# First loads in half pieces, sums of the opening moved from TensorE to VectorE, and a new order of the set-up block in a causal convolution

## Chip, cores, metric

One core of a Trainium2 chip. The metric is the device time of one launch in microseconds (us). A kernel was run 3 to 9 times beside runs of the kernel before on the same chip. The groups of experiments below ran on different chips, so each is compared with its own runs of the kernel before. Medians are given with their range, and ratios with a 95% interval.

## The reference

A causal convolution over the sequence with 8 taps, each a full 512x512 matrix:

```python
# x: (8, 4096, 512) fp32, kernel: (8, 512, 512) fp32
out = np.zeros_like(x)
for k in range(8):
    shifted = x if k == 0 else np.concatenate(
        [np.zeros((B, k, D), dtype=np.float32), x[:, :-k, :]], axis=1)
    out += np.matmul(shifted, kernel[k])
```

## The kernel before

Sequence positions are cut into 128 runs of 256, one run per partition; eight steps of all runs make one block. Instead of 8 taps x 8 steps = 64 matrix products per block, three levels of sums and differences of rows and of weights bring it down to three "nodes" of 9 products of 128x512x512, each product 4 matmuls of 128x512, 216 ns each. From here on "a product" is one such matmul of 128x512. Each node after the first begins with a copy by ScalarE, its "opening copy", by which progress is read below. From about 100 us on a steady loop runs, one node in 7.774 us, TensorE without gaps. The change leaves that loop alone.

The first 100 us are another matter. The weights and the first blocks have to arrive, and there are no sums of weights yet. So the first node (block 0, lower half) is computed directly with 64 matmuls, while loads come in one after another through the GpSimd queue (fp32 in memory, bf16 on chip). The order of every instruction is set by hand. The parts that matter, with cuts marked:

```python
    def load(out, src):
        nc.gpsimd.dma_start(out=out, in_=src)
    ...
    load(H[1:P, 4:8], xr[0:P - 1, RUN - 4:RUN, :])   # history: last 4 rows of the run before
    load_x(0, 0)                                     # first x block, rows 0 to 3
    ident = spool.tile([P, P], bf, name="ident")
    make_identity(nc, ident)                         # GpSimd: a memset and a select
    identh = ...; identn = ...                       # GpSimd: two more helpers, 0.9 us
    ...
    for r in range(2):                               # 16 matmuls on zeros: warm the array
        for k in range(4):
            fill(pair(k))
    ...
    load_w(4)
    transpose_pe("xh", 2, H, 5, 8)
    sums_pe("d4a", 1, (-4, 0), (-3, 1))   # transposes and adds in one go: matmuls that
    ...                                   # accumulate x and history rows in PSUM
    transpose_pe("x1", 2, xin[0, 1], 0, 4)
    nc.scalar.copy(out=XT[:, 4:8], in_=bank["x1"])   # x block two, evicted by ScalarE
```

A `bank` is a buffer in PSUM, into which TensorE writes here; to evict it is to copy it to SBUF. "x block two" is `xin[0, 1]`, "block three" `xin[1, 0]`; the later x tiles are transposed by DMA instead of TensorE. D4, E4 and the like are names of sums of rows; "the D4 sum behind the DMA transpose" is VectorE's first add on a tile transposed by DMA. The "warming matmuls" are the 16 on zeros.

## Time and profile before

| | before |
|---|---|
| time | 783.48 us median of 3 (783.41 to 783.87) |
| span in the profile | 780.9 us |
| first product starts | 13.81 us |
| x block two's transposes start | 25.08 us |
| 120 products done, next one starts | 48.79 us |
| 160 products done (opening copy of the fifth node) | 57.7 us |
| an opening copy early in the loop | 89.4 us |

The busy shares, the stretches, the start of TensorE's timeline and two load issues are shown in the prediction.

GpSimd's timeline at the start (start us, duration us, engine, line, what). L80 is the line of every load issue: history at 1.23, x at 1.90, then work on the identity and its helpers, then the first weights at 4.04.

```profile
1.23 0.68 POOL L80 DMA_DIRECT2D D<-in_x_dram  x1 [0.80 <-POOLq L637]
1.90 0.56 POOL L80 DMA_DIRECT2D xin<-in_x_dram  x1
...
3.53 0.54 POOL L148 TENSOR_SCALAR identn<-ident 128x128 bf16<-128x128 bf16 x1
4.04 0.82 POOL L80 DMA_DIRECT2D w<-in_kernel_dram  x1
```

### The profile page before, as it was taken

What the parts mean: (1) busy time and instruction counts of PE and PEld (TensorE: products, weight loads), DVE (VectorE), ACT (ScalarE), POOL (GpSimd) and SP (SyncE); (2) the same over time, 40 slices, a digit from 0 to 9 for tenths busy, and PEclk for the clock granted to TensorE, in tenths of its full rate; (3) what the DMA queues carried; (4) which work ended last, traced back from release to release, by engine and by line L of the source; (5) the groups of instructions that cost most, each with busy time, mean ns of one, the idle gap of its engine ahead of it and who ended that gap; (6) DMA issues with size and microseconds to landing.
All of it is one profiled execution on the core that took longest, in us unless ns stands there. A gap on an engine that the chain in (4) does not pass through costs nothing.

```text
span 780.9 us, 9507 instructions
## 1 busy us (share of the span) xinstructions
PE 767.4 (98%) x3620; PEld 349.0 (45%) x3620; DVE 659.3 (84%) x764; ACT 283.2 (36%) x460; POOL 42.8 (5%) x83
## 2 busy tenths in 40 slices
PE   7899999999999999999999999999999999999997
PEld 4444444444444444444444444444444444444443
DVE  4899888888888889888898888898888898888895
ACT  2453433333333333343324343333343333343332
POOL 5000000000000000000000000000000000000000
PEclk9999999999999999999999999999999999999999
DMA  9963979778788777878777788877787877788753
GB/s 163 210 120 114 237 176 207 169 187 167 178 179 206 174 176 173 177 184 194 184 171 168 179 190 188 191 166 179 165 187 187 195 170 182 166 172 200 179 153 123
DMA packets 159229, 138.37 MB, mean 177 GB/s; under 512 B 130130, under 2 KB 134226, under 8 KB 159184
## 3 DMA queue, kind: packets, MB, share of 16 engines
q1 hardware_dynamic: 145312, 98.84, 46.3%
q0 software_dynamic: 13728, 38.66, 31.1%
q8 instruction: 28, 0.46, 0.2%
q10 hardware_dynamic: 144, 0.26, 0.1%
q14 instruction: 17, 0.14, 0.1%
HBM read 77.32 MB, written 67.11 MB: 185 GB/s over the span
## 4 chain that ended last, share of the span: by engine, by line
PE 94%; DMA 3%; DVE 1%; POOL 1%; issue 0%; ACT 0%; DVEq 0%; POOLq 0%
PE pp L215 94%; DMA xin<-in_x_dram 2%; DMA XT<-xin 1%; POOL w L80 0%; DVE D L76 0%; PE pp L192 0%; DVE pp L76 0%; ACT XT L390 0%; DVE y L76 0%; POOL D L80 0%; DVEq L648 0%; POOL xin L80 0%; POOL identn L148 0%; PE pp L186 0%; POOL ident masks.py:199 0%
## 5 line engine op out<-in xcount | busy, mean ns | idle before, releaser
L215 PE MATMUL pp<-w,D 128*128 128x512 bf16 x3280 | 715.8, 379 | 1.7 <-DMA w<-in_kernel_dram 0.9
L215 PEld LDWEIGHTS <-D 128*128 128x128 bf16 x3280 | 320.2, 98 | 390.4 <-issue 2.8
L76 DVE TENSOR_TENSOR D<-D 128x2048 bf16<-128x2048 bf16 (+2 forms) x250 | 227.2, 948 | 3.4 <-ACT D L369 3.4
L76 DVE TENSOR_TENSOR y<-pp,ms 128x1024 f32<-128x1024 f32 (+1 forms) x121 | 146.4, 1212 | 45.3 <-PE pp L215 45.3
L76 DVE TENSOR_TENSOR D<-XT 128x2048 bf16<-128x2048 bf16 (+2 forms) x153 | 142.5, 947 | 12.1 <-DMA XT<-xin 10.4
L262 ACT COPY pp<-pp 128x512 f32<-128x512 f32 x95 | 54.1, 570 | 260.6 <-PE pp L215 260.6
L274 ACT COPY pp<-pp 128x512 f32<-128x512 f32 x95 | 54.2, 570 | 167.1 <-PE pp L215 165.6
L76 DVE TENSOR_TENSOR pp<-dts,pp 128x512 f32<-128x512 f32 x95 | 65.7, 691 | 43.9 <-ACT dts L280 42.6
L317 ACT COPY ms<-pp 128x1024 f32<-128x1024 f32 x60 | 61.0, 1016 | 35.0 <-PE pp L215 33.0
L80 POOL DMA_DIRECT2D xin<-in_x_dram x64 | 34.0, 531 | 692.5 <-DMA XT<-xin 675.8
L290 DVE SCALAR_TENSOR_TENSOR pp<-pp,dts 128x512 f32<-128x512 f32 x95 | 66.0, 695 | 3.2
L280 ACT COPY dts<-pp 128x512 f32<-128x512 f32 x95 | 57.5, 606 | 0.0
L276 ACT ACTIVATE pp<-pp 128x512 f32<-128x512 f32 x95 | 56.1, 590 | 0.8 <-PE pp L215 0.8
L215 PE MATMUL pp<-w,XT 128*128 128x512 bf16 x120 | 30.8, 379 | 0.0
L76 DVE TENSOR_TENSOR w<-w,w 128x2048 bf16<-128x2048 bf16 x19 | 22.9, 1219 | 1.5 <-DMA w<-in_kernel_dram 1.3
L215 PEld LDWEIGHTS <-XT 128*128 128x128 bf16 x120 | 11.7, 98 | 14.2
L186 PE MATMUL pp<-zero,ident 128*128 128x512 bf16 x20 | 6.7, 493 | 3.1 <-POOL ident masks.py:199 3.1
L215 PE MATMUL pp<-w,F 128*128 128x512 bf16 x36 | 8.7, 379 | 0.2 <-DVE pp L76 0.2
L215 PE MATMUL pp<-w,w 128*128 128x512 bf16 x36 | 8.3, 379 | 0.0
L192 PE MATMUL pp<-ident,xin 128*128 128x128 bf16 x48 | 3.2, 219 | 3.6 <-DMA xin<-in_x_dram 1.4
L80 POOL DMA_DIRECT2D w<-in_kernel_dram x8 | 6.1, 785 | 0.5 <-DMA w<-in_kernel_dram 0.5
L358 DVE COPY D<-pp 128x1536 bf16<-128x1536 bf16 x1 | 1.0, 958 | 6.1 <-PE pp L192 6.1
(59 smaller groups left out, 78.7 us busy)
## 6 DMA issues: line engine op xcount, KB each, us to landing
out_dram<-y SPq DMA_DIRECT2D x123, 512.0 KB, 3.4
xin<-in_x_dram POOLq DMA_DIRECT2D x64, 512.0 KB, 6.0
w<-in_kernel_dram POOLq DMA_DIRECT2D x8, 512.0 KB, 15.7
out_dram<-ms SPq DMA_DIRECT2D x2, 512.0 KB, 5.4
out_dram<-f SPq DMA_DIRECT2D x2, 512.0 KB, 6.3
XT<-xin SPq DMA_TRANSPOSE x61, 6.1
D<-in_x_dram POOLq DMA_DIRECT2D x1, 508.0 KB, 5.6
D<-in_x_dram POOLq DMA_DIRECT2D x1, 381.0 KB, 9.4
```

Of the source, the lines that this page charges most:

```text
L76: nc.vector.tensor_tensor(out=o, in0=a, in1=b, op=op)
L80: nc.gpsimd.dma_start(out=out, in_=src)
L186: nc.tensor.matmul(pw[:, h], lhsT=ident, rhs=zero, start=True, stop=True)
L192: nc.tensor.transpose(o[:, t - t0, c * P:(c + 1) * P], src[:, t, c * P:(c + 1) * P], ident)
L215: nc.tensor.matmul(bank, lhsT=comp[:, c * P:(c + 1) * P], rhs=w[:, c, :], start=start and c == 0, stop=c == DC - 1, skip_group_check=True)
L262: nc.scalar.copy(out=n.q[:, 0], in_=n.q[:, 1])
L274: nc.scalar.copy(out=n.p[b_][:, 1], in_=n.q[:, 1])
L276: nc.scalar.mul(out=n.p[b_][:, 1], in_=n.q[:, 1], mul=-1.0)
L280: nc.scalar.copy(out=n.dts, in_=n.q[:, 0])
L290: nc.vector.scalar_tensor_tensor(out=p[:, 0], in0=p[:, 1], scalar=-1.0, in1=n.dts, op0=MUL, op1=SUB)
L317: nc.scalar.copy(out=ms[b_], in_=p)
L358: nc.vector.tensor_copy(out=XF[:, 0:3], in_=bank["xh"])
```

## The change

The intent: start the first products sooner, and take work off TensorE. The first history rows and the first x block are loaded in two halves each, so that their transposes can begin when half has come. TensorE only transposes; VectorE makes the sums that TensorE made by accumulating. The two helper identities are not needed any more. The rest of the set-up block (some 200 calls) is put in a new order. The core of the diff:

```diff
-    load(H[1:P, 4:8], xr[0:P - 1, RUN - 4:RUN, :])
-    load_x(0, 0)
+    load_h(-4, -2)
+    load_x(0, 0, 0, 2)
     ident = spool.tile([P, P], bf, name="ident")
     make_identity(nc, ident)
-    identh = spool.tile([P, P], bf, name="identh")
-    ... (identh, identn made on GpSimd)
 ... (cut: mid_pe, mid_act, sums_pe removed)
+    transpose_pe("h0", 0, H, 4, 6)
+    load_h(-2, 0)
+    load_x(0, 0, 2, 4)
     load_w(4)
-    transpose_pe("xh", 2, H, 5, 8)
-    sums_pe("d4a", 1, (-4, 0), (-3, 1))
+    transpose_pe("x0", 2, xin[0, 0], 0, 2)
+    nc.vector.tensor_copy(out=XF[:, 4:6], in_=bank["x0"])
+    nc.vector.tensor_copy(out=XF[:, 0:2], in_=bank["h0"])
+    first_run(XF[:, 0:2])
+    tt(D4[:, 0:2], XF[:, 0:2], XF[:, 4:6], ADD)
 ...
     transpose_pe("x1", 2, xin[0, 1], 0, 4)
-    nc.scalar.copy(out=XT[:, 4:8], in_=bank["x1"])
+    nc.vector.tensor_copy(out=XT[:, 4:8], in_=bank["x1"])
 ... (cut: the other calls of the block in a new order)
```

More of the change, by code (lines that the diff above doesn't have):

```diff
@@ L82, with load_x @@
     xin = {}
-    def load_x(i, h):
-        xin[i, h] = xpool.tile([P, 4, D], bf, name="xin")
-        load(xin[i, h], xr[:, K * i + 4 * h:K * i + 4 * h + 4, :])
+    def load_x(i, h, a=0, b=4):
+        if a == 0:
+            xin[i, h] = xpool.tile([P, 4, D], bf, name="xin")
+        t0 = K * i + 4 * h
+        load(xin[i, h][:, a:b], xr[:, t0 + a:t0 + b, :])
     def transpose_x(i, h):
@@ L138, with load_h @@
     H = D421
-    load(H[1:P, 4:8], xr[0:P - 1, RUN - 4:RUN, :])
-    load_x(0, 0)
+    def load_h(a, b):
+        load(H[1:P, 8 + a:8 + b], xr[0:P - 1, RUN + a:RUN + b, :])
+    load_h(-4, -2)
+    load_x(0, 0, 0, 2)
     ident = spool.tile([P, P], bf, name="ident")
     make_identity(nc, ident)
-    identh = spool.tile([P, P], bf, name="identh")
-    nc.gpsimd.tensor_copy(out=identh, in_=ident)
-    nc.gpsimd.memset(identh[:, 0:P:G], 0.0)
-    identn = spool.tile([P, P], bf, name="identn")
-    nc.gpsimd.tensor_scalar_mul(out=identn, in0=ident, scalar1=-1.0)
     zero = spool.tile([P, D], bf, name="zero")
@@ L170 @@
     bank = {}
-    def mid_pe(h, k, *which):
-        o, u, v = mid(*which)
-        bank[which, h] = pair(k)
-        for c in range(2):
-            pw = bank[which, h][:, c]
-            nc.tensor.matmul(pw, lhsT=ident, rhs=u[:, 2 * h + c], start=True, stop=False)
-            nc.tensor.matmul(pw, lhsT=identn, rhs=v[:, 2 * h + c], start=False, stop=True)
-    def mid_act(h, *which):
-        nc.scalar.copy(out=mid(*which)[0][:, 2 * h:2 * h + 2], in_=bank[which, h])
     def fill(pw):
@@ L194, in transpose_pe @@
         bank[name] = o[:, 0:t1 - t0]
-    def sums_pe(name, k, *sums):
-        pw = bank[name] = pair(k)
-        for h, ts_ in enumerate(sums):
-            for c in range(DC):
-                for n, t in enumerate(ts_):
-                    src, idt = (xin[0, 0][:, t], ident) if t >= 0 else (H[:, 8 + t], identh)
-                    nc.tensor.matmul(pw[:, h, c * P:(c + 1) * P], lhsT=src[:, c * P:(c + 1) * P],
-                                     rhs=idt, start=n == 0, stop=n == len(ts_) - 1,
-                                     skip_group_check=True)
     for r in range(2):
@@ L346, with first_run @@
     C0, C1 = W[MID, HI, MID], W[MID, LO, MID]
-    load_w(4)
-    transpose_pe("xh", 2, H, 5, 8)
-    sums_pe("d4a", 1, (-4, 0), (-3, 1))
-    load(H[1:P, 1:4], xr[0:P - 1, RUN - 7:RUN - 4, :])
+    def first_run(z):
+        nc.vector.memset(z[:, :, 0:D:G], 0.0)
+    transpose_pe("h0", 0, H, 4, 6)
+    load_h(-2, 0)
+    load_x(0, 0, 2, 4)
+    load_w(4)
+    transpose_pe("x0", 2, xin[0, 0], 0, 2)
+    nc.vector.tensor_copy(out=XF[:, 4:6], in_=bank["x0"])
+    nc.vector.tensor_copy(out=XF[:, 0:2], in_=bank["h0"])
@@ L356 @@
+    first_run(XF[:, 0:2])
+    tt(D4[:, 0:2], XF[:, 0:2], XF[:, 4:6], ADD)
+    transpose_pe("xb", 2, xin[0, 0], 2, 4)
+    n0.p = {0: pair(0), 1: pair(1)}
+    transpose_pe("h1", 0, H, 6, 8)
+    nc.scalar.copy(out=XF[:, 6:8], in_=bank["xb"])
+    nc.scalar.copy(out=XF[:, 2:4], in_=bank["h1"])
+    direct(0, 0)
+    load_h(-7, -4)
+    first_run(XF[:, 2:4])
     load_w(6)
-    sums_pe("d4b", 2, (-2, 2), (-1, 3))
-    nc.vector.tensor_copy(out=XF[:, 0:3], in_=bank["xh"])
-    transpose_pe("xf", 2, xin[0, 0], 0, 4)
+    transpose_pe("he", 2, H, 1, 4)
@@ L360 @@
     load_w(5)
-    nc.vector.tensor_copy(out=D4[:, 0:2], in_=bank["d4a"])
-    nc.scalar.copy(out=D4[:, 2:4], in_=bank["d4b"])
-    n0.p = {0: pair(0), 1: pair(1)}
+    tt(D4[:, 2:4], XF[:, 2:4], XF[:, 6:8], ADD)
+    direct(0, 3)
+    direct(0, 1)
+    nc.scalar.copy(out=F0, in_=XF[:, 4])
     fill(pair(3))
-    load_w(7)
-    direct(0, 2)
-    direct(0, 1)
-    direct(0, 3)
-    nc.scalar.copy(out=XF[:, 3:7], in_=bank["xf"])
-    sums_pe("e4a", 2, (-5, -1), (-6, -2))
-    nc.vector.memset(XF[:, 0:3, 0:D:G], 0.0)
@@ L372 @@
-    tt(D2, XF[:, 0:5], XF[:, 2:7], ADD)
-    direct(2, 3)
-    tt(F21, D2[:, 0:4], D2[:, 1:5], ADD)
-    mid_dve(1, LO, HI)
-    sums_pe("e4b", 2, (-7, -3))
-    direct(1, 2)
-    direct(0, 0)
-    load_x(0, 1)
-    tt(D1, XF[:, 2:4], XF[:, 3:5], ADD)
-    mid_dve(2, LO, HI)
-    nc.scalar.copy(out=E4[:, 3:1:-1], in_=bank["e4a"])
-    mid_dve(2, LO, LO)
-    load_x(1, 0)
-    load_w(0)
-    nc.vector.tensor_copy(out=E4[:, 1], in_=bank["e4b"][:, 0])
-    direct(1, 3)
-    direct(1, 1)
-    transpose_pe("x1", 2, xin[0, 1], 0, 4)
@@ L390 @@
-    nc.scalar.copy(out=XT[:, 4:8], in_=bank["x1"])
-    load_w(2)
-    mid_dve(1, LO, LO)
-    direct(1, 0)
-    transpose_pe("x2", 2, xin[1, 0], 0, 4)
-    mid_dve(2, LO, MID)
-    load_w(1)
-    tt(D4[:, 4:8], XF[:, 3:7], XT[:, 4:8], ADD)
-    direct(2, 1)
-    nc.vector.tensor_copy(out=XT[:, 2:4], in_=bank["x2"][:, 2:4])
+    direct(0, 2)
+    direct(2, 2)
+    tt(E4[:, 1:4], bank["he"], XF[:, 1:4], ADD)
+    first_run(E4[:, 1:4])
+    tt(D2, XF[:, 1:6], XF[:, 3:8], ADD)
+    load_w(7)
+    direct(1, 0)
@@ new lines @@
+    direct(1, 3)
+    load_x(0, 1)
+    tt(D1, XF[:, 3:5], XF[:, 4:6], ADD)
+    direct(1, 2)
+    mid_dve(1, LO, HI)
+    load_x(1, 0)
+    direct(1, 1)
+    mid_dve(2, LO, HI)
+    tt(F21, D2[:, 0:4], D2[:, 1:5], ADD)
+    load_w(0)
+    mid_dve(1, LO, LO)
+    mid_dve(2, LO, LO)
+    direct(2, 3)
+    mid_dve(2, LO, MID)
+    transpose_pe("x1", 2, xin[0, 1], 0, 4)
+    nc.vector.tensor_copy(out=XT[:, 4:8], in_=bank["x1"])
+    tt(D4[:, 4:8], XF[:, 4:8], XT[:, 4:8], ADD)
+    direct(2, 0)
+    nc.scalar.copy(out=C0[:, 0:2], in_=XT[:, 6:8])
@@ L400 @@
+    prep_d41(HI)
+    transpose_pe("x2", 2, xin[1, 0], 0, 4)
+    nc.scalar.copy(out=XT[:, 2:4], in_=bank["x2"][:, 2:4])
+    load_w(2)
+    direct(3, 0)
     prep_d42(HI)
     nc.scalar.copy(out=XT[:, 0:2], in_=bank["x2"][:, 0:2])
-    nc.scalar.copy(out=C0[:, 0:2], in_=XT[:, 6:8])
+    direct(3, 3)
     tt(T4, XT[:, 4:8], XT[:, 0:4], ADD)
     direct(3, 1)
-    prep_d41(HI)
-    tt(T42[:, 0:2], D4[:, 6:8], T4[:, 0:2], ADD)
-    direct(3, 0)
-    nc.scalar.copy(out=C1, in_=XT[:, 0:4])
-    direct(2, 0)
@@ L410 @@
-    nc.scalar.copy(out=F0, in_=XF[:, 3])
-    direct(3, 3)
-    fill(pair(2))
-    tt(D41[:, 1], T4[:, 0], T4[:, 1], ADD)
-    load_w(3)
+    fill(pair(2))
+    load_w(3)
+    nc.scalar.copy(out=C1, in_=XT[:, 0:4])
+    direct(3, 2)
+    tt(D41[:, 1], T4[:, 0], T4[:, 1], ADD)
+    node_a1(1)
+    tt(D41[:, 0], D4[:, 7], T4[:, 0], ADD)
+    direct(2, 1)
+    load_w(1)
+    node_a0(nodes[1])
+    tt(T42[:, 0:2], D4[:, 6:8], T4[:, 0:2], ADD)
     tt(T42[:, 2:4], T4[:, 0:2], T4[:, 2:4], ADD)
-    node_a1(1)
@@ L417 @@
-    direct(2, 2)
+    node_u(nodes[1])
+    load_x(1, 1)
+    tt(D421[:, 0], D42[:, 7], T42[:, 0], ADD)
     node_e(nodes[0], 0)
-    tt(D41[:, 0], D4[:, 7], T4[:, 0], ADD)
-    node_a0(nodes[1])
-    node_u(nodes[1])
-    direct(3, 2)
+    node_seed(nodes[1], 0)
     mid_dve(1, HI, HI)
-    node_seed(nodes[1], 0)
     prep_d27()
+    node_v(nodes[1], 0)
+    mid_dve(2, HI, LO)
+    tt(D421[:, 1:4], T42[:, 0:3], T42[:, 1:4], ADD)
+    node_seed(nodes[1], 1)
     node_dts(nodes[1])
-    node_seed(nodes[1], 1)
@@ L428 @@
     tt(D42[:, 3], D4[:, 1], D4[:, 3], ADD)
-    node_v(nodes[1], 0)
-    tt(D421[:, 0], D42[:, 7], T42[:, 0], ADD)
-    load_x(1, 1)
-    node_v(nodes[1], 1)
-    tt(D421[:, 1:4], T42[:, 0:3], T42[:, 1:4], ADD)
-    node_a1(2)
-    mid_dve(2, HI, LO)
-    transpose_x(1, 1)
-    mid_dve(1, HI, LO)
-    node_d(nodes[1], 0)
-    node_l(nodes[1], 0, LO)
-    mid_dve(2, HI, MID)
-    nc.scalar.copy(out=D4[:, 2:4], in_=T4[:, 2:4])
-    node_d(nodes[1], 1)
-    load_x(2, 1)
-    node_e(nodes[0], 1)
-    node_u(nodes[2])
@@ L446 @@
-    node_l(nodes[1], 0, HI)
-    node_e(nodes[1], 0)
-    node_a0(nodes[2])
-    node_seed(nodes[2], 0)
-    prep_d421(HI)
-    load_x(2, 0)
-    mid_dve(2, HI, HI)
-    node_l(nodes[1], 1, LO)
-    node_l(nodes[1], 1, HI)
-    nc.scalar.copy(out=U1, in_=XT[:, 0])
+    load_x(2, 0)
+    node_d(nodes[1], 0)
+    mid_dve(1, HI, LO)
+    mid_dve(2, HI, HI)
+    node_a1(2)
+    node_l(nodes[1], 0, HI)
+    node_v(nodes[1], 1)
+    load_x(2, 1)
+    node_d(nodes[1], 1)
+    mid_dve(2, HI, MID)
+    prep_d421(HI)
@@ L456 @@
+    node_l(nodes[1], 0, LO)
+    node_a0(nodes[2])
+    node_l(nodes[1], 1, HI)
+    node_e(nodes[1], 0)
+    node_e(nodes[0], 1)
+    nc.scalar.copy(out=D4[:, 2:4], in_=T4[:, 2:4])
+    node_u(nodes[2])
+    mid_dve(0, HI, HI)
+    node_seed(nodes[2], 0)
+    node_seed(nodes[2], 1)
+    node_l(nodes[1], 1, LO)
+    node_dts(nodes[2])
+    transpose_x(1, 1)
+    nc.scalar.copy(out=D42[:, 3], in_=T42[:, 3])
     node_v(nodes[2], 0)
+    node_v(nodes[2], 1)
     prep_d4(HI)
-    nc.scalar.copy(out=D42[:, 3], in_=T42[:, 3])
@@ L459 @@
-    node_seed(nodes[2], 1)
-    node_v(nodes[2], 1)
-    node_dts(nodes[2])
-    mid_dve(0, HI, HI)
-    node_e(nodes[1], 1)
     prep_d41(HI)
     node_d(nodes[2], 0)
-    node_l(nodes[2], 0, HI)
-    tt(A1[:, 0], C0[:, 1], C1[:, 0], ADD)
-    prep_d42(HI)
-    node_d(nodes[2], 1)
-    transpose_x(2, 0)
-    mid_dve(0, LO, HI)
     node_a1(3)
     node_l(nodes[2], 0, LO)
+    mid_dve(0, LO, LO)
+    mid_dve(0, HI, LO)
+    prep_d42(HI)
+    node_l(nodes[2], 0, HI)
     node_a0(nodes[3])
+    node_d(nodes[2], 1)
@@ L475 @@
+    node_u(nodes[3])
     node_e(nodes[2], 0)
-    mid_dve(0, LO, LO)
+    node_e(nodes[1], 1)
+    node_seed(nodes[3], 0)
     tt(D421[:, 0:4], D42[:, 3:7], D42[:, 4:8], ADD)
-    node_u(nodes[3])
     node_l(nodes[2], 1, HI)
     node_seed(nodes[3], 1)
-    node_seed(nodes[3], 0)
+    mid_dve(0, LO, HI)
+    tt(A1[:, 0], C0[:, 1], C1[:, 0], ADD)
     node_dts(nodes[3])
+    node_v(nodes[3], 0)
+    node_v(nodes[3], 1)
     mid_dve(1, MID, HI)
-    node_v(nodes[3], 1)
+    node_l(nodes[2], 1, LO)
@@ L485 @@
     node_d(nodes[3], 1)
-    mid_dve(0, HI, LO)
-    node_v(nodes[3], 0)
+    node_e(nodes[2], 1)
     node_d(nodes[3], 0)
-    node_l(nodes[2], 1, LO)
+    mid_dve(1, MID, LO)
     node_a1(4)
-    mid_dve(1, MID, LO)
-    tt(D21[:, 2:4], C1[:, 0:2], C1[:, 2:4], ADD)
     node_l(nodes[3], 1, HI)
     node_l(nodes[3], 0, LO)
+    nc.scalar.copy(out=U1, in_=XT[:, 0])
+    node_a0(nodes[4])
+    tt(D21[:, 2:4], C1[:, 0:2], C1[:, 2:4], ADD)
     mid_dve(2, MID, MID)
-    node_e(nodes[2], 1)
-    load_x(3, 0)
@@ L498 @@
-    node_l(nodes[3], 0, HI)
-    node_a0(nodes[4])
-    tt(D21[:, 0:2], C0[:, 0:2], C1[:, 0:2], ADD)
-    node_u(nodes[4])
-    node_e(nodes[3], 0)
-    node_l(nodes[3], 1, LO)
-    tt(A1[:, 1], C1[:, 0], C1[:, 1], ADD)
+    node_dts(nodes[4])
+    tt(D21[:, 0:2], C0[:, 0:2], C1[:, 0:2], ADD)
+    node_l(nodes[3], 0, HI)
+    node_e(nodes[3], 0)
+    node_u(nodes[4])
+    tt(A1[:, 1], C1[:, 0], C1[:, 1], ADD)
+    node_l(nodes[3], 1, LO)
+    load_x(3, 0)
+    transpose_x(2, 0)
     mid_dve(2, MID, LO)
+    node_seed(nodes[4], 0)
@@ L506 @@
+    node_seed(nodes[4], 1)
+    node_v(nodes[4], 0)
     mid_dve(2, MID, HI)
-    node_seed(nodes[4], 0)
-    node_v(nodes[4], 0)
-    node_seed(nodes[4], 1)
-    node_dts(nodes[4])
+    node_a1(5)
     node_d(nodes[4], 0)
-    node_a1(5)
     node_v(nodes[4], 1)
+    node_l(nodes[4], 0, HI)
     prep_m()
-    node_l(nodes[4], 0, HI)
     node_l(nodes[4], 0, LO)
+    node_e(nodes[3], 1)
+    node_u(nodes[5])
+    node_d(nodes[4], 1)
     node_a0(nodes[5])
-    node_e(nodes[3], 1)
-    node_d(nodes[4], 1)
@@ L520 @@
-    node_u(nodes[5])
+    node_y(nodes[4], 0, LO)
+    node_y(nodes[4], 0, HI)
+    prep_d4(LO)
+    node_l(nodes[4], 1, HI)
+    tt(F21[:, 1], D21[:, 0], D21[:, 1], ADD)
+    node_dts(nodes[5])
+    tt(F21[:, 0], D2[:, 0], D21[:, 0], ADD)
     node_seed(nodes[5], 0)
     node_l(nodes[4], 1, LO)
-    tt(F21[:, 0], D2[:, 0], D21[:, 0], ADD)
-    node_l(nodes[4], 1, HI)
-    node_y(nodes[4], 0, LO)
-    node_y(nodes[4], 0, HI)
+    node_v(nodes[5], 0)
+    node_y(nodes[4], 1, LO)
     store(0, LO, 0, first[0, LO, 0])
-    tt(F21[:, 1], D21[:, 0], D21[:, 1], ADD)
@@ L529 @@
-    node_dts(nodes[5])
-    node_v(nodes[5], 0)
+    store(0, HI, 0, first[0, HI, 0])
+    node_d(nodes[5], 0)
     prep_d27()
     node_seed(nodes[5], 1)
-    store(0, HI, 0, first[0, HI, 0])
-    load_x(3, 1)
-    node_y(nodes[4], 1, LO)
     node_v(nodes[5], 1)
-    node_d(nodes[5], 0)
+    node_a1(6)
     node_d(nodes[5], 1)
+    transpose_x(2, 1)
+    node_y(nodes[4], 1, HI)
+    store(0, HI, 1, first[0, HI, 1])
+    node_l(nodes[5], 0, HI)
+    node_l(nodes[5], 0, LO)
     tt(F21[:, 2:4], D21[:, 1:3], D21[:, 2:4], ADD)
-    node_l(nodes[5], 0, LO)
@@ L541 @@
-    node_l(nodes[5], 0, HI)
-    node_a1(6)
-    node_l(nodes[5], 1, HI)
+    node_y(nodes[5], 0, HI)
     node_u(nodes[6])
-    prep_d4(LO)
-    store(0, LO, 1, first[0, LO, 1])
-    node_y(nodes[4], 1, HI)
-    node_a0(nodes[6])
     node_y(nodes[5], 0, LO)
     prep_d41(LO)
-    transpose_x(2, 1)
+    node_l(nodes[5], 1, HI)
     node_l(nodes[5], 1, LO)
-    store(0, HI, 1, first[0, HI, 1])
+    store(0, LO, 1, first[0, LO, 1])
     node_seed(nodes[6], 0)
+    node_a0(nodes[6])
     node_v(nodes[6], 0)
-    node_y(nodes[5], 0, HI)
@@ L557 @@
     tt(D21[:, 0:2], D2[:, 0:2], D2[:, 1:3], ADD)
-    node_dts(nodes[6])
+    store(1, LO, 0, first[1, LO, 0])
     node_seed(nodes[6], 1)
     node_v(nodes[6], 1)
+    node_dts(nodes[6])
+    prep_d42(LO)
+    node_d(nodes[6], 0)
+    store(1, HI, 0, first[1, HI, 0])
+    node_y(nodes[5], 1, HI)
+    node_a1(7)
+    load_x(3, 1)
+    node_y(nodes[5], 1, LO)
+    store(1, HI, 1, first[1, HI, 1])
+    store(1, LO, 1, first[1, LO, 1])
     tt(D21[:, 2:4], D2[:, 2:4], D2[:, 3:5], ADD)
-    node_d(nodes[6], 0)
@@ L563 @@
-    prep_d42(LO)
-    node_y(nodes[5], 1, HI)
     node_d(nodes[6], 1)
-    store(1, LO, 0, first[1, LO, 0])
-    node_y(nodes[5], 1, LO)
-    store(1, HI, 0, first[1, HI, 0])
-    node_a1(7)
-    store(1, HI, 1, first[1, HI, 1])
     prep_d4(HI)
-    store(1, LO, 1, first[1, LO, 1])
     for k, (i, a) in enumerate(order):
```

## The prediction

> **What bounds the kernel now.** I read the busy shares first, then a table of stretches, then the timeline of the first 50 us with its waits, and last the landings of single loads.
>
> ```profile
> PE 767.4 (98%) x3620; PEld 349.0 (45%) x3620; DVE 659.3 (84%) x764; ACT 283.2 (36%) x460; POOL 42.8 (5%) x83
> ```
>
> TensorE looks busy 98% of 780.9 us, but the average hides two regimes. The table of stretches shows them (columns: stretch and length, busy us and count of each engine, clock, DMA share, GB/s):
>
> ```profile
> 0.00:13.80 13.80, 9.51 (x78) 5.67 (x79) 4.36 (x5) 2.52 (x3) 6.97 (x17) 1.00 0.85 147
> 13.80:36.00 22.20, 18.57 (x126) 9.67 (x125) 17.78 (x20) 9.91 (x9) 4.62 (x7) 1.00 1.20 207
> 36.00:60.00 24.00, 23.26 (x107) 10.22 (x106) 23.48 (x28) 13.52 (x21) 1.06 (x2) 1.00 0.75 135
> ...
> 120.00:200.00 80.00, 80.00 (x372) 36.22 (x371) 69.39 (x80) 27.87 (x47) 3.70 (x7) 1.00 0.82 186
> ```
>
> From 120 us on TensorE has no gap. ScalarE's copy that opens a node (36 products of 128x512, 95 such nodes plus a first one of 64 products) comes every 7.774 us there: 216 ns a product, which nothing in this change touches. The code has 3,484 products (the trace lost 12), and 3,484 x 0.216 = 752.5 us. So 780.9 - 752.5 = 28.4 us are not products: about 4.4 us after the last one (the critical chain leaves TensorE at about 776.4), about 24 us before and between the first ones. Only these 24 us can move.
>
> The timeline shows where they lie (start us, us, engine, line; L215 are products, L192 transposes; in brackets the idle time before and what ended it):
>
> ```profile
> 8.45 0.83 PE L192 MATMUL pp<-ident,D 128*128 128x128 bf16 x12
> ...
> 13.81 2.75 PE L215 MATMUL pp<-w,D 128*128 128x512 bf16 x12
> ...
> 20.07 3.61 PE L215 MATMUL pp<-w,D 128*128 128x512 bf16 x16 [0.91 <-DMA w<-in_kernel_dram]
> ...
> 25.08 1.07 PE L192 MATMUL pp<-ident,xin 128*128 128x128 bf16 x16 [1.40 <-DMA xin<-in_x_dram]
> ...
> 26.18 1.86 ACT L390 COPY XT<-pp 128x2048 bf16<-128x2048 bf16 x1 [7.68 <-PE pp L192]
> ...
> 28.10 1.05 PE L192 MATMUL pp<-ident,xin 128*128 128x128 bf16 x16 [1.09 <-ACT XT L390]
> ```
>
> ```profile
> 45.17 1.23 DVE L76 TENSOR_TENSOR D<-XT 128x2048 bf16<-128x2048 bf16 x1 [0.52 <-DMA XT<-xin]
> ```
>
> ```profile
> 48.79 12.28 PE L215 MATMUL pp<-w,D 128*128 128x512 bf16 x56 [0.74 <-DVE pp L76]
> ```
>
> The first product starts at 13.8 us. Up to 28 us TensorE waits for loads and for ScalarE's 1.86 us eviction. From 28 to about 90 us VectorE is packed (23.48 of 24 us in one stretch) and sets the pace with TensorE; at 45.17 even VectorE waits for a DMA transpose. By 48.79 us TensorE has done 120 products, worth 25.9 us: 22.9 of the 24 us are lost by then.
>
> The loads have their own clock. Issues looked at singly (KB written, us to landing):
>
> ```profile
> D<-in_x_dram POOLq DMA_DIRECT2D x1, 508.0 KB, 5.6
> ```
>
> ```profile
> w<-in_kernel_dram POOLq DMA_DIRECT2D x1, 512.0 KB, 8.5
> ```
>
> The history rows are issued at 1.23 and land at 6.8; the first x block lands at 9.4, the first weights (issued 4.04) at 12.5, the next at 16.8, then 20.1, 22.6, x block two at 25.0, three at 27.5, and so on every 2.5 us to 40.2. One load after another, at the full 205 GB/s written: a stream that the change does not shorten.
>
> **What the Trainium skill says.**
> - "TensorE: Matmul & The Clock Gate", section "Wait — 56ns, not 53.3ns?", gives 55.6 ns start to start for 128 columns and 215.7 ns for 512 on a warm array. The trace agrees: 16 transposes in 1.05 us of which the last takes 0.219 are 55 ns apart, and a product takes 216.
> - The same page, "Part 4: PE-mode transpose", says that transposes do not count as busy for the clock gate in the way matmuls do. No run here shows it yet; it carries a rival below.
> - "VectorE: DVE Perf Modes", "The perf-mode tier table": an add of two bf16 tensors in SBUF runs at 2x (1224 ns for 2048), with any PSUM operand at 1x. The trace has 1220 ns for 128x2048.
> - "Perfetto Trace Analysis", "DMA Optimizations": splitting a transfer lets work start sooner if the DMA engines are generally idle. Here they are idle only before 3 us; the share is 0.85 to 1.20 after that, so halves bring forward the first half and nothing else.
>
> **The change part by part.**
>
> (a) Removed: 56 sum matmuls (32 for D4, 24 for E4) and 28 transposes; added: 44 transposes. 84 - 44 = 40 fewer, at 0.055 each 2.2 us of TensorE, but mostly beside waits. The two helper identities on GpSimd go (0.9 us of POOL); two more load issues of 0.6 us take their place, so the first weights are issued at about 4.3 instead of 4.0 and still land at 12.5, behind the same bytes.
>
> (b) First product. The 16 warming matmuls end at 8.2 as before. The first history half (landed by about 5.6) and first x half (6.8) are there: 16 transposes to 9.5. VectorE copies two banks of 128x1024 (0.68 each) to 10.8, then adds 128x1024 (0.69) by 12.0. The second halves transpose at 10.3 to 11.4; ScalarE evicts both (1.01 each, 0.92 apart) by 12.85, and the first product's bank is the one evicted last. Weights 12.5, eviction 12.85: first product at 12.9, 0.9 us earlier.
>
> (c) To 28.6 us. After four products (13.8) the older history rows, landing at 14.25, hold TensorE 0.5 us; 12 transposes end at 15.0; sixteen products and two fills (3.9 us) end at 18.9; the next need weights that land at 20.1: 1.2 us idle. Twenty products to 24.4, idle to 25.08 for x block two, transposes to 26.15, four products. Its eviction moves from ScalarE (1.86) to VectorE (about 1.2), done at 27.5, so the third block's transposes start when it lands, 27.55, not at 28.10, and end at 28.6, not 29.15. By then 44 products are done against 36: 8 x 0.216 + 0.55 = 2.3 us ahead.
>
> (d) What survives. Now VectorE binds. It has one 1.2 us eviction more and one 0.68 copy less, and reaches the sum T4 at 30.65 (when ScalarE's last eviction lands) against 30.99, with one 0.6 us sum already behind it. TensorE spends about 1 us waiting for ScalarE's seeds of node 1, since no product stands between "u" and the first "v" any more. VectorE's D4 sum on the DMA transpose again cannot start before 45.2 (the same load at 40.2 plus 5.0). But one 1.14 us weight difference has been moved in front of that gate. So the operand for the next product is there at about 47.7 instead of 48.75, and 128 products are done at 48.9 against 50.5: 1.6 ahead. The next weight difference needed (1,MID,HI) ends at 55.4, and TensorE, there at 54.9, waits: 40 groups of four are done at 56.3 against 57.7, 1.4 ahead.
>
> (e) 57 to 97 us. The transpose of block 2 is issued later, at about 57.5, and is due by 63.4; with 5 to 6 us it just fits. The kernel before loses 0.16, 0.36 and 0.24 us there to VectorE; the new order gives VectorE's results 1 us or more of slack, so 0 to 0.5 comes back. After 97 us the loop and the tail are the same.
>
> Sum: 1.4 + about 0.1 = 1.5 us. 783.5 - 1.5 = 782.0 us.
>
> **Rivals.**
> - The gates bind harder than I think: VectorE or the 45.2 us transpose leaves nothing, and the 2.3 us of part (c) become waiting. For it: VectorE's 23.48 of 24 us. Against it: the 1.14 us moved in front of the gate. Time 783.2 to 783.6.
> - The array goes cold. From 8.2 to 12.9 us TensorE now does only transposes and waits. At half speed for some 3.4 us (the window that the page's Part 1 gives), eight products would cost 1.7 us more. Against it: 1.7 us of waits at 20.1 and 25.1 absorb most. Time 782 to 783.5.
> - A later wait appears: the block 2 transpose lands after 64 and stops VectorE, which then delays its later sums. Time 782.5 to 784.
> - The new order fits better than my walk: no seed wait, no wait at 55, and the 2.3 us stay to the end. Time 781.
>
> **Range and chances.** The first and last rivals bound the range: 780.8 to 783.5, with 782.0 as the likeliest. 2% is 15.7 us; all losses before the loop are 24 us, and the first 12.5 of them are the load of x and weights that stays, so faster by 2% is nearly impossible, and nothing in the change can add 15 us. Chances 0.01, 0.98, 0.01.
>
> **What would show it.** First product at 12.9; waits of about 1.2 us for weights at 20.1 and 0.6 for x at 25.1; third block's transposes at 27.55; VectorE's D4 sum at 45.2 behind the DMA transpose; 128 products by 49; the nodes' opening copies in the loop about 1.5 us earlier than in the trace before; a loop of 7.774 us per node. First products paced at 430 ns, as the first warming matmuls are, a VectorE gap near 63 us, or a changed loop pace would make it wrong.

## More of the kernel before

A stretch of 2 us (busy us and counts of PE, PEld, DVE, ACT, POOL, then clock, DMA share, GB/s). The last figure matters: 207 GB/s, loads at full pace.

```profile
6.00:8.00 2.00, 2.00 (x8) 0.81 (x7) 0.00 (x0) 0.00 (x0) 2.00 (x4) 1.00 1.06 207
```

The chain of waits that ends last, in order of time (start us, length us, what). Up to 25 us it is made of the issue of x block two and its way through the queue (17.42 us behind the loads ahead of it); from 29 us it is TensorE with one detour by VectorE.

```profile
7.61 17.42 DMA xin<-in_x_dram
...
25.08 1.08 PE pp L192 x16
...
29.15 4.32 PE pp L215 x20
...
33.90 13.30 PE pp L215 x60
```

## The result, and the profile after

| | before | after |
|---|---|---|
| time, median (range) | 783.65 us (783.41 to 783.91, 6 runs) | 783.74 us (782.96 to 784.59, 6 runs) |
| first product | 13.81 | 13.63 |
| first weights have landed | 12.54 | 13.40 |
| x block two's transposes | 25.08 | 26.46 |
| x block three's transposes | 28.10 | 28.92 |
| D4 sum behind the DMA transpose | 45.17 | 46.69 |
| 120 products done, next starts | 48.79 | 48.77 |
| 160 products done | 57.7 | 58.2 |
| the opening copy that was at 89.4 | 89.4 | 89.8 |

The ratio of the times is 1.0002, with 0.9989 to 1.0015 as its interval: the same, and 1.7 us above what I predicted. Ratios here and below are the mean time of one kernel's fast runs over that of the other's fast runs of the same rounds, so they are not quite the ratio of the medians quoted. The profiled run of the changed kernel was its slowest, so its span (782.7) overstates it; what is read below lies in its first 110 us.

The busy shares show the intent fulfilled and nothing gained. TensorE has 40 operations fewer: 3,580 weight loads for 3,620, as the code has it (of the matmuls, some records are missing in this trace).

```profile
PE 764.5 (98%) x3509; PEld 347.7 (44%) x3580; DVE 660.8 (84%) x768; ACT 280.7 (36%) x459; POOL 42.8 (5%) x82
```

The chain of waits of the changed kernel, in order of time, is the key view. The same load of x block two, issued at the same time (7.55 against 7.61), takes 18.86 us instead of 17.42. And where the kernel before had TensorE on the chain from 29 us on, now it is a load again until 41.5, the DMA transpose behind it, and VectorE's sum.

```profile
7.55 18.86 DMA xin<-in_x_dram
...
26.46 1.08 PE pp L180 x16
...
27.82 13.69 DMA xin<-in_x_dram
...
41.60 5.00 DMA XT<-xin
...
46.69 1.24 DVE D L76
```

Where did the stream lose its time? Among the 2 us stretches one stands out: 118 GB/s instead of 207.

```profile
6.00:8.00 2.00, 2.00 (x6) 0.76 (x5) 0.00 (x0) 0.00 (x0) 2.00 (x4) 1.00 0.81 118
```

I added up the sizes of the load queue's packets in the order in which they ended: 512 KB are in at 6.65 us (before 6.43), but 1,024 KB at 10.15 (before 8.86): of 1.29 us, 0.22 are lost in the first half megabyte and the rest in the second, which is now the second pair of halves. Their 255 packets start between 6.4 and 10.34 us, and around 6.6 us only 9 packets are in flight on the 16 DMA engines, where before it was 16. GpSimd issued these two loads at 2.99 and 3.53, right after the identity:

```profile
2.44 0.23 POOL masks.py:197 MEMSET ident<- 128x128 bf16 x1
2.75 0.29 POOL masks.py:199 TENSOR_SCALAR_AFFINE_SELECT ident<-ident 128x128 bf16<-128x128 bf16 x1
2.99 0.55 POOL L80 DMA_DIRECT2D D<-in_x_dram  x1
3.53 0.55 POOL L80 DMA_DIRECT2D xin<-in_x_dram  x1
```

The first weights come next in the queue. They are issued at 4.07, as before (4.04), and land 9.3 us later, at 13.40, where before it was 8.5 us (shown in the prediction) and 12.54:

```profile
w<-in_kernel_dram POOLq DMA_DIRECT2D x1, 512.0 KB, 9.3
```

TensorE's start shows a second thing (L192 are products now, L180 transposes). Eight products from 16.66 take 2.88 us where a warm array needs 1.9, and twelve transposes take 1.46 instead of 0.83: the array had gone cold. The table of stretches says it in one figure, the clock 0.92, which was 1.00 in this stretch before; the trace's clock record is at one half from 15.24 to 18.66 us.

```profile
13.63 1.02 PE L192 MATMUL pp<-w,D 128*128 128x512 bf16 x3 [1.42 <-ACT D L346]
15.41 1.46 PE L180 MATMUL pp<-ident,D 128*128 128x128 bf16 x12 [0.76 <-DMA D<-in_x_dram]
16.66 2.88 PE L192 MATMUL pp<-w,D 128*128 128x512 bf16 x8
```

```profile
13.80:36.00 22.20, 20.31 (x116) 10.22 (x118) 19.10 (x23) 6.07 (x7) 3.20 (x5) 0.92 1.19 207
```

At 107.83 a third thing: VectorE waited 2.14 us for a DMA transpose that took 6.8 us from issue to landing (100.94 to 107.74), and TensorE lost 1.1 us behind it, at 109.5. In the trace before the same transpose took 5.0 us. The line before, then the line after:

```profile
105.65 1.23 DVE L76 TENSOR_TENSOR D<-XT 128x2048 bf16<-128x2048 bf16 x1 [0.35 <-DMA XT<-xin]
...
107.83 1.23 DVE L76 TENSOR_TENSOR D<-XT 128x2048 bf16<-128x2048 bf16 x1 [2.14 <-DMA XT<-xin]
```

So there were three candidates for the missing 1.5 us: the loads (my theory after reading), the cold array (a rival of the prediction), and VectorE's added work (another). The experiments test them. The late transpose is a fourth; no experiment was made for it, but the traces of all of them bear on it (see the rivals below).

### The profile page after: what moved, and what is told of

Its sections match the earlier page's. It is cut to its first block, busy times and chain, and to the rows that moved or that the text cites. A ratio compares the mean times of both kernels' runs of the same rounds, so it can differ in the third digit from the quotient of the medians.

```text
span 782.7 us, 9358 instructions
## 1 busy us (share of the span) xinstructions
PE 764.5 (98%) x3509; PEld 347.7 (44%) x3580; DVE 660.8 (84%) x768; ACT 280.7 (36%) x459; POOL 42.8 (5%) x82
## 4 chain that ended last, share of the span: by engine, by line
PE 87%; DMA 7%; DVE 4%; issue 1%; POOL 1%; ACT 0%; SPq 0%; DVEq 0%; ACTq 0%; POOLq 0%
PE pp L192 87%; DMA xin<-in_x_dram 4%; DMA XT<-xin 2%; DVE D L76 1%; DVE w L76 1%; DVE y L76 1%; POOL w L80 0%; DVE pp L76 0%; DVE pp L267 0%; ACT pp L251 0%; POOL D L80 0%; POOL xin L80 0%; PE pp L180 0%; DVE A L76 0%; SPq L277 0%
## 5 line engine op out<-in xcount | busy, mean ns | idle before, releaser
L192 PE MATMUL pp<-w,D 128*128 128x512 bf16 x3214 | 714.0, 379 | 7.1 <-ACT D L346 1.4
L192 PEld LDWEIGHTS <-D 128*128 128x128 bf16 x3280 | 320.5, 98 | 393.7 <-issue 5.1
L76 DVE TENSOR_TENSOR D<-D 128x1024 bf16<-128x1024 bf16 x252 | 228.5, 946 | 0.4 <-issue 0.2
L192 PE MATMUL pp<-w,XT 128*128 128x512 bf16 x117 | 30.5, 379 | 0.2
L192 PEld LDWEIGHTS <-XT 128*128 128x128 bf16 x120 | 11.7, 98 | 14.2
L192 PE MATMUL pp<-w,w 128*128 128x512 bf16 x35 | 9.0, 379 | 0.7 <-ACT pp L251 0.7
L192 PE MATMUL pp<-w,F 128*128 128x512 bf16 x35 | 8.4, 379 | 0.0
```

The costliest lines, as they stand in the source:

```text
L76: nc.vector.tensor_tensor(out=o, in0=a, in1=b, op=op)
L192: nc.tensor.matmul(bank, lhsT=comp[:, c * P:(c + 1) * P], rhs=w[:, c, :], start=start and c == 0, stop=c == DC - 1, skip_group_check=True)
```

## The experiments

Twelve kernels ran, in three groups of four; all gave correct results. "Block two" is the start of x block two's transposes, "160" the start of the opening copy of the fifth node (160 products done), "6–8" the GB/s in that stretch, all from the one profiled run of each. The names e1 to e12 are those that the expectations use; the medians of the kernel before were 783.51, 783.33 and 783.42 us in the three groups.

| kernel | median us (range) | ratio to before, interval | 6–8 | block two | 160 |
|---|---|---|---|---|---|
| before | 783.5 | 1 | 207 | 25.08 | 57.7 |
| after | 783.74 (782.96–784.59) | 1.0002 [0.9989, 1.0015] | 118 | 26.46 | 58.2 |
| after again (e5) | 784.11 (782.86–784.62) | 1.0009 [0.9997, 1.0022] | 101 | 26.60 | 57.8 |
| after, whole loads (e1) | 782.24 (781.81–782.59) | 0.9984 [0.9972, 0.9997] | 199 | 25.81 | 57.0 |
| before, with halves (e2) | 784.44 (783.54–784.9) | 1.0012 [0.9999, 1.0025] | 160 | 26.29 | 59.2 |
| after, array kept warm (e3) | 783.47 (783.05–783.57) | 0.9999 [0.9987, 1.0012] | 108 | 26.07 | 57.8 |
| after, all halves issued first (e4) | 782.62 (781.8–783.99) | 0.9989 [0.9976, 1.0003] | 199 | 25.28 | 56.4 |
| e4 with memsets between (e9) | 783.8 (783.42–784.14) | 1.0006 [0.999, 1.0023] | 126 | 26.15 | 57.9 |
| after, identity before the loads (e6) | 782.42 (782.19–783.72) | 0.9995 [0.9982, 1.0008] | 181 | 25.48 | 56.8 |
| before, block two evicted by VectorE (e7) | 785.45 (784.48–785.69) | 1.0024 [1.001, 1.0037] | 207 | 24.91 | 60.0 |
| e4 with 8 warming matmuls (e8) | 781.92 (781.62–782.23) | 0.9984 [0.9971, 0.9996] | 184 | 25.77 | 56.9 |
| e8 again (e12) | 781.85 (781.55–783.54) | 0.9984 [0.9969, 0.9999] | 188 | 25.35 | 56.5 |
| e6 with 8 warming matmuls (e10) | 782.43 (782.18–782.69) | 0.9987 [0.9972, 1.0002] | 161 | 26.04 | 57.4 |
| e1 with 8 warming matmuls (e11) | 781.98 (781.53–783.08) | 0.9984 [0.9969, 0.9998] | 203 | 25.66 | 57.1 |

**Group one: which part costs?** First the halves alone undone, everything else as changed:

```diff
-    load_h(-4, -2)
-    load_x(0, 0, 0, 2)
+    load_h(-4, 0)
+    load_x(0, 0)
 ...
-    load_h(-2, 0)
-    load_x(0, 0, 2, 4)
```

> The changed kernel with its first history and x rows loaded whole again, all else as changed. Theory 1 (the halves made the whole load stream 1.4 us later, and that ate the gain): x block two lands near 25.1 us instead of 26.5, the first DMA transpose starts near 40.2 instead of 41.6, the D4 sum behind it near 45.2 instead of 46.7, and the time falls by 1.0 to 1.5 us to 782.2 to 782.8. Rival A (the cold TensorE array costs it): time unchanged, 783.5 to 784. Rival B (VectorE's packed order costs it, wherever the loads land): loads land earlier, but the time stays at 783.5 to 784.

The time is 782.24 us, and the stream is whole again (199 GB/s). The chain of waits now has no second load on it: after block two's transposes comes VectorE, and it stays on the chain down to the D4 sum at 45.40, with no wait for a DMA named any more. Block two itself starts at 25.81, only 0.65 us before the changed kernel's and still 0.7 behind the kernel before, so the stretch from 6 to 8 us is not the whole of its delay.

```profile
25.81 1.08 PE pp L180 x16
...
26.91 1.24 DVE XT L378
...
28.17 1.24 DVE D L76
...
45.40 1.23 DVE D L76
```

Then the opposite: the halves alone, put into the kernel before.

```diff
-    load(H[1:P, 4:8], xr[0:P - 1, RUN - 4:RUN, :])
-    load_x(0, 0)
+    load(H[1:P, 4:6], xr[0:P - 1, RUN - 4:RUN - 2, :])
+    load_x(0, 0, 0, 2)
 ... (identity, identh, identn)
+    load(H[1:P, 6:8], xr[0:P - 1, RUN - 2:RUN, :])
+    load_x(0, 0, 2, 4)
     load_w(4)
```

> The kernel before with one thing changed: its first history and x rows loaded in halves. Theory 1: x block two lands 1.2 to 1.6 us later than 25.0 and the time rises by 1.0 to 1.6 us to 784.7 to 785.3. Rivals A and B: the halves are harmless by themselves, 783.4 to 783.9.

784.44 against 783.51 for the kernel before of the same rounds: 0.9 us lost, a little less than expected and with an interval that just reaches 1; block two is 1.2 us later. Both kernels tell the same story from two sides: the halves, as they are issued here, cost about 0.9 us in the kernel before and 1.5 in the changed one (medians of different rounds), and the rest of the change gains about 1.3. Which part of that rest gains it was not separated.

Third, the array kept warm, by 14 more matmuls on zeros in the gaps where the changed kernel waits:

```diff
     tt(D4[:, 0:2], XF[:, 0:2], XF[:, 4:6], ADD)
+    for _ in range(2):
+        fill(pair(3))
     transpose_pe("xb", 2, xin[0, 0], 2, 4)
 ... (3 more before direct(0, 0), 2 more after it)
```

> The changed kernel with 14 more matmuls on zeros in TensorE's three early gaps (10.0, 12.0 and 14.3 us), so that the array stays at full speed. Rival A: the products from 13.6 to 18.7 us go at 216 ns instead of 430, and the time falls by 1 us or more, to below 782.8. Theory 1: they go at 216 ns too, but then TensorE waits about 1.5 us longer for the weights and x block two, and the time stays within 0.3 us of the changed kernel, 783.4 to 784.1.

The edit does what it should, and the time stays at 783.47. The eight products take 1.89 us and the twelve transposes 0.83, and then TensorE waits for a load, which the cold kernel did not need to:

```profile
15.45 0.83 PE L180 MATMUL pp<-ident,D 128*128 128x128 bf16 x12
16.12 1.89 PE L192 MATMUL pp<-w,D 128*128 128x512 bf16 x8
...
21.31 1.02 PE L192 MATMUL pp<-w,w 128*128 128x512 bf16 x4 [1.15 <-DMA w<-in_kernel_dram]
```

The speed won is handed back 3 us later. The cold array was real and cost nothing measurable.

Fourth, the same four half loads, but all issued before the identity is made:

```diff
     load_h(-4, -2)
     load_x(0, 0, 0, 2)
+    load_h(-2, 0)
+    load_x(0, 0, 2, 4)
     ident = spool.tile([P, P], bf, name="ident")
     make_identity(nc, ident)
```

> The changed kernel with all four half loads issued before GpSimd makes the identity, so the third and fourth issue 0.6 us earlier. In the trace half of the DMA engines are idle from 6.2 to 7.2 us. If that is because the third load was issued too late, the gap closes, x block two lands near 25.9 instead of 26.5 and the time falls by about 0.5 us; if the gap has another cause or the halves are slow by their packets alone (2 KB packets took 180 ns, half of a 4 KB packet 162 ns), it lands at 26.3 to 26.6 and the time stays at 783.5 to 784.

```profile
2.45 0.55 POOL L80 DMA_DIRECT2D D<-in_x_dram  x1
2.98 0.54 POOL L80 DMA_DIRECT2D xin<-in_x_dram  x1
3.51 0.22 POOL masks.py:197 MEMSET ident<- 128x128 bf16 x1
```

The stream is back at 199 GB/s, 1,024 KB are in at 9.03 us (8.86 with whole loads), block two starts at 25.28 and 160 products are done at 56.4, 1.8 us before the changed kernel. So it is not the size of the pieces: a half load's packets of 2 KB took 174 to 192 ns where the whole load's of 4 KB took 324 to 333. It is where they are issued. The time, 782.62, is better, but one of its runs was at 783.99 and the interval just reaches 1.

**Group two: is it the place of the identity?** First the changed kernel once more, unedited, for the noise.

> The changed kernel once more, unedited, beside the next three on one chip. Is the slow stretch of its load stream (118 GB/s from 6 to 8 us, against 199 to 207 with whole loads) there in another execution? Theory 1: yes, within 100 to 165 GB/s, x block two lands at 26 us or later, and the time is 783.4 to 784.0. Rival: it was one execution's accident; then 190 GB/s or more, and x block two near 25.3.

784.11 us; the stretch, at 101 GB/s, is as poor as the first time. This time the array was warm without help (eight products in 1.89 us), and the time was no better for it, which is a second, unplanned answer to the cold array:

```profile
16.18 1.89 PE L192 MATMUL pp<-w,D 128*128 128x512 bf16 x8
```

Second, the identity made before any load:

```diff
-    load_h(-4, -2)
-    load_x(0, 0, 0, 2)
     ident = spool.tile([P, P], bf, name="ident")
     make_identity(nc, ident)
+    load_h(-4, -2)
+    load_x(0, 0, 0, 2)
```

> The changed kernel with the identity made before any load is issued, so that all four half loads are issued in a row, about 0.8 us later than in the run that issued them first. If the slow stretch comes from GpSimd's identity work standing between the second and third issue, it is gone (190 GB/s or more in every 2 us stretch once the loads run), and x block two lands near 26.1, 0.8 later than there. If it comes from half loads being too small to keep the queue fed, it is there again and x block two lands at 26.8 or later. Time 783.2 to 784.2 either way; the trace decides, not the time.

The four half loads are issued about 0.2 us later than with the halves first (I had expected 0.8), but without a break; the stretch has 181 GB/s, block two starts at 25.48, and the time is 782.42, against 784.11 for the unedited kernel in the same rounds. Two of my figures were missed: the stretch stays under 190 GB/s, and the time is below 783.2. The spread of both is wide (783.72 the slowest here, 782.86 the fastest there), so this one pair settles it in the trace rather than in the time.

Third, one part of the change alone in the kernel before: block two's bank evicted by VectorE.

```diff
     transpose_pe("x1", 2, xin[0, 1], 0, 4)
-    nc.scalar.copy(out=XT[:, 4:8], in_=bank["x1"])
+    nc.vector.tensor_copy(out=XT[:, 4:8], in_=bank["x1"])
```

> The kernel before with one part of the change alone: x block two's bank of 128x2048 is evicted by VectorE (about 1.2 us) instead of ScalarE (1.86 us). If the gain that whole loads set free comes from this shorter path to block three's transposes, they start at 27.6 instead of 28.1 and the time falls by 0.4 to 0.6 us, to 782.9 to 783.2. If VectorE's packed stretch takes it back (it has 1.1 us more to do there), the time stays or rises, 783.4 to 784.2.

785.45 us, 2 us slower, and slower than either case that I had allowed for (784.2 at most). In VectorE's timeline the eviction is quick, but in the old order two weight differences stand before the sum that uses it, and TensorE waits 2.09 us for that sum's followers:

```profile
26.02 1.22 DVE L390 COPY XT<-pp 128x2048 bf16<-128x2048 bf16 x1 [1.77 <-PE pp L192]
27.16 2.47 DVE L76 TENSOR_TENSOR w<-w,w 128x2048 bf16<-128x2048 bf16 x2
29.55 1.22 DVE L76 TENSOR_TENSOR D<-D,XT 128x2048 bf16<-128x2048 bf16 x1
```

```profile
35.27 4.45 PE L215 MATMUL pp<-w,D 128*128 128x512 bf16 x12 [2.09 <-DVE D L76]
```

In the old order the move costs time. The new order puts that sum right behind the copy (28.17 behind 26.91 in the kernel with whole loads, shown above); whether it would do as well there with ScalarE's eviction, no run shows.

Fourth, the halves issued first, and 8 instead of 16 warming matmuls (`range(2)` becomes `range(1)`), since they, not the loads, had held back the first transposes:

> The run with the four half loads issued first, with 8 instead of 16 warming matmuls in front, so that the first half loads can be transposed as soon as they land. If the halves are worth something and the warming matmuls hide it, the first product starts 1 us or more earlier and the time falls by 0.5 us or more against that run (782.6). If the loads that follow set the pace, the first product starts near 13 as before and the time is 782.3 to 783.0.

781.92 us, all five runs between 781.62 and 782.23, with an interval wholly below 1; the unedited changed kernel of the same rounds ran at 782.86 to 784.62. The first product starts at 12.79 (13.99 in e4), and the time is 0.7 us under e4's, in other rounds: by the measure that I had set, this spoke for the halves. The last pair below tests that directly and answers no.

**Group three: any work, or the identity's? And are halves worth anything?** The kernel with all halves first, with two idle memsets put in the place where the identity had been:

```diff
     load_h(-4, -2)
     load_x(0, 0, 0, 2)
+    idle = spool.tile([P, P], bf, name="idle")
+    for _ in range(2):
+        nc.gpsimd.memset(idle, 0.0)
+    load_h(-2, 0)
+    load_x(0, 0, 2, 4)
     ident = spool.tile([P, P], bf, name="ident")
```

> All four half loads issued before the identity is made, as in e4, but with two GpSimd memsets of a 128x128 tile between the second and the third load. If any GpSimd work in that place makes the slow stretch: 6 to 8 us falls to 165 GB/s or less, x block two's transposes start at 26 us or later, time 783.3 to 784.1. If it takes the affine select (or what goes with it): 180 GB/s or more, x block two at 25.3 to 25.8, time 782.2 to 783.0.

```profile
2.44 0.49 POOL L148 MEMSET idle<- 128x128 bf16 x2
2.88 0.54 POOL L80 DMA_DIRECT2D D<-in_x_dram  x1
```

```profile
41.26 5.02 DMA XT<-xin
...
46.37 1.24 DVE D L76
```

The slow stretch is back (126 GB/s), the DMA transpose is back on the chain of waits ahead of the D4 sum, and so is the time: 783.8. The third issue is only 0.43 us later than without the memsets (2.88 for 2.45), but 1,024 KB are in 0.90 us later (9.93 for 9.03). This is the cleanest pair, for the memsets compute nothing that anyone uses. But they do two things at once: they occupy GpSimd, and they delay the third and all later issues by 0.43 us. The pair does not separate the two.

The identity first, with 8 warming matmuls, asks whether an unbroken row of issues is enough:

> The identity made before any load, as in e6, with 8 instead of 16 warming matmuls. If nothing between the issues is what keeps the loads whole, the stream is as in e8 but some 0.2 us later: x block two at 25.3 to 25.9, time 781.7 to 782.6. If it was the order of issue alone (loads first) that helped in e8: 783 or more.

The time is as expected (782.43), the trace is not: 161 GB/s in the stretch and block two at 26.04, later than the 25.9 that I allowed. With nothing between the issues the stream still dipped somewhat in this run. So a break filled with work is one thing that thins the stream, not the only one, and the start of block two varies by about half a microsecond between runs with equal issues (25.48 and 26.04 here, 25.35 and 25.77 for the halves first).

Put in order of the time of the third issue, the changed kernels with halves gave from 6 to 8 us: issued at 2.45, 199, 184 and 188 GB/s; at 2.65, 181 and 161; at 2.88, 126; at 3.00, 118, 101 and 108. By this row, the lateness alone would do as a cause, without the work; no run has a break with nothing in it. And the kernel before with halves (e2) fits neither account: its third issue comes at 4.03, behind five GpSimd operations, and it has 160 GB/s and 1,024 KB in at 9.40. What is shown is the remedy, not the mechanism.

The last two differ only in halves or whole loads, both with 8 warming matmuls:

> First history and x loaded whole (as e1), with 8 instead of 16 warming matmuls. If half loads are worth something once the warming matmuls no longer hide them, this is slower than e12 by 0.5 us or more. If the loads that follow set the pace, and the first products' start is hidden, the two are the same within 0.4 us: 781.6 to 782.4.

> e8 once more, beside e11 on the same chip: 781.6 to 782.4, x block two at 25.3 to 25.9.

781.98 and 781.85 us, with ranges of 1.6 and 2.0 us that overlap almost wholly. With halves the first product starts at 12.73 us, with whole loads at 13.73, and this microsecond is worth nothing measurable: the loads behind it come when they come. The halves, which gave the change its name, neither gain nor need to lose anything that these runs can measure. In the trace with halves the array was cold as well, and that run took 781.74 us, among the fastest of all:

```profile
15.61 2.95 PE L194 MATMUL pp<-w,D 128*128 128x512 bf16 x8
```

## Why the prediction was wrong

**What failed: "a stream that the change does not shorten", taken as a stream that stays the same.** In part (a) I wrote that the first weights are issued a little later "and still land at 12.5, behind the same bytes". They landed at 13.40. I counted the bytes and the issue times, and did not ask whether the engines would find packets to work on. Undivided, the first two loads are one megabyte, enough to feed them to 8.9 us; halved, they are half a megabyte, used up at 6.65, and what follows had been issued after a break in the row of issues. The stream had lost 1.3 us by the end of the first megabyte, and the later loads stayed behind: block two at 26.46 instead of the 25.08 in part (c), block three's transposes at 28.92 instead of 27.55, the DMA transpose issued at 41.60 instead of 40.2, and the D4 sum that part (d) has at 45.2 at 46.69. At the opening copy at 89.4 us the changed kernel is 0.35 us behind the kernel before, where I had it 1.5 ahead; with whole loads it is 0.9 ahead, and with halves issued first and 8 warming matmuls (e12) 1.4 ahead. The pace of the loop is 7.77 to 7.78 us a node in all three, as predicted.

**The sum of the gain was nearly right.** Part (d) wanted 128 products by 48.9 us against 50.5 before. With whole loads the product after the 120th starts at 47.48, which makes 47.48 + 8 x 0.216 = 49.2; in the changed kernel it starts at 48.77, which makes 50.5, exactly the kernel before. The wait for a weight difference that I put near 55 us is there (TensorE loses 0.28 us twice between 52 and 57). With halves issued first (e12) it starts at 47.01, which makes 48.7. 160 products: predicted 56.3, with whole loads 57.0, in the changed kernel 58.2. And the times: predicted 782.0, with whole loads 782.24, with halves issued first and fewer warming matmuls 781.92 and 781.85. None of these is the kernel that was predicted, so this supports the sum of the rest of the change, and not the prediction. The fewer-warming runs also lack the late transpose, of which I had no account.

**First product.** Predicted 12.9, measured 13.63. Two terms were off. The warming matmuls ended at about 9.2 us, and not at 8.2 (8.45 in the trace before), because the array's switch to its full pace came later in this run (the kernel before reached it after 6.9 us, the changed one after 8.2). And the first weights landed at 13.40, so even with an earlier switch the product could not have started before that. With 8 warming matmuls and the stream whole it is 12.73, with the weights in at 12.59. The start was mis-sized by 0.7 us, and it doesn't matter, as the last pair shows.

**The rivals.** "The gates bind harder" gave nearly the right time (783.2 to 783.6 for 783.74 measured) for another reason: I had VectorE in mind, or a transpose at 45.2 that left no room, and it was the load ahead of the transpose. "The array goes cold" happened in one of the two profiled runs of the changed kernel, at about its predicted price (five products and twelve transposes at half speed, 5 x 0.21 + 0.63 = 1.7 us), and was absorbed as the "against" of that rival said; the warm kernel, at the same time, shows it. The array was cold in e12 too, at no cost that its time shows. "A later wait" came true, near 108 us and not at 64, and I had no run made for it. In all seven traces with the new order and 16 warming matmuls a DMA transpose issued near 100 us takes 6.3 to 6.9 us and VectorE waits 1.7 to 2.2 us for it; TensorE loses 0.3 to 1.1 us behind that (1.1 in both traces of the changed kernel, 0.3 with whole loads). In the three traces with the old order and the four with 8 warming matmuls the same transpose takes 5.0 us, VectorE waits 0.4 us or less, and TensorE loses nothing there. So this goes with the kernel and is hardly chance from run to run: in both profiled runs it is a part of the changed kernel's loss, beside the stream. Both were among the slowest of their kernel, and whether its faster runs, which left no trace, have it too is not known. It also blurs every comparison of 8 with 16 warming matmuls. Why it goes with the warming matmuls is open. The stream's share can be read in front of it: at the opening copy at 89.4 us the kernel with whole loads is 1.3 us ahead of the changed one (88.47 against 89.76). The line of e12, to be held against 107.83 above:

```profile
103.72 1.22 DVE L76 TENSOR_TENSOR D<-XT 128x2048 bf16<-128x2048 bf16 x1 [0.38 <-DMA XT<-xin]
```

**What stays open.** Why a break between the issues thins the stream, and whether it is the work in it or only the lateness. It is not work of VectorE, which runs nothing from 3.3 to 7.7 us in any of these traces and the same memsets before that in all of them. The Trainium skill, "DMA: Bandwidth & Descriptors", section "SWDGE vs HWDGE vs iDMA", says that for loads issued from GpSimd its own cores compute the descriptors before a DMA engine moves anything. That would fit a supply that falls behind when those cores have just done something else, but the trace doesn't show descriptors. It shows two pictures: fewer packets in flight (9 for 16, in the changed kernel), and, with the memsets, as many as ever, but slow ones (348 ns on average for 2 KB between 6 and 7 us, where it took 192 without the memsets). The run with the warm array (e3), whose loads are issued as in the changed kernel, shows the second picture: 16 to 18 in flight, at 547 ns on average. So one order of issue gave both pictures. And a milder dip came once with nothing between the issues.

## What to carry to other kernels

When a large load is split, try the pieces in one unbroken row (here that restored what the halves had lost), and look at what the issuing engine does between them, and at the GB/s of the stretch in which the first pieces run out. Where loads come in one stream, being early at its head is worth nothing unless the end of the stream moves too; follow the last load on the chain of waits, not the first. And moving one step to a faster engine can cost time by itself (2 us here) if the order of that engine's other work stays. Compare the late stretches too: here a wait near 108 us, long after the first loads, was in half of the traces, and no part of the prediction had looked for it there.

## What the Trainium skill lacked or had wrong

- "DMA: Bandwidth & Descriptors", section "SWDGE vs HWDGE vs iDMA", describes how GpSimd builds descriptors, but not what GpSimd's other work does to that supply. Here two memsets of a 128x128 tile between the second and the third of four issues brought the stretch from 6 to 8 us from 199 down to 126 GB/s (and the third issue from 2.45 to 2.88 us); a memset and a select gave 118, 101 and 108 in three runs.
- "Perfetto Trace Analysis", section "DMA Optimizations", has splitting for idle DMA engines and larger transfers for throughput. It lacks the middle case seen here: halves cost next to nothing by size (2 KB packets 174 to 192 ns, 4 KB packets 324 to 333; 1,024 KB in at 9.03 against 8.86 us), yet in the changed kernel, where the pieces weren't issued together, they were in 1.3 us later (10.15).
- "VectorE: DVE Perf Modes", section "The perf-mode tier table", puts an add with any PSUM operand at 1x, while "Why PSUM operands drop a tier" on the same page keeps 1x to fp32. The run sides with the latter: the changed kernel's E4 sum, with one bf16 operand in PSUM, ran as fast as the same size with both in SBUF: 0.96 against 0.95 us.

```profile
16.91 0.96 DVE L76 TENSOR_TENSOR w<-pp,D 128x1536 bf16<-128x1536 bf16 x1 [2.21 <-PE pp L180]
...
38.07 0.95 DVE L76 TENSOR_TENSOR D<-w 128x1536 bf16<-128x1536 bf16 x1
```
